# An MLP by Strassen's seven products on one Trainium2 core: the first product also in seven, the hidden layer through DRAM, the second summed over all of K in PSUM

## The chip, the cores and the metric

The kernel runs on one core of a Trainium2 chip. [...] SP's queue (SyncE) issues nearly all DMAs. The metric is device time in us. Each profile tells the span of the instructions; the execution's time is a little longer.

## The reference, cut to what matters

One layer of a hybrid decoder: three token mixers side by side, an output projection, and an MLP. All of it before the MLP stays as it is, so only the end matters:

```
x  = x + y @ w_out[l]                                        # x: 1024 tokens x 1024
hm = rms_norm(x, mlp_norm[l])
x  = x + jnp.square(jax.nn.relu(hm @ mlp_w1[l])) @ mlp_w2[l]  # w1: 1024 x 4096, w2: 4096 x 1024
```

## The kernel before

Every fp32 operand of a matmul is split into a high part (a cast to fp32r, on ScalarE) and a low part (the rest, a subtraction on VectorE or GpSimd). A product is then three matmuls: high x high, high x low, low x high.

The hidden layer's 4096 columns are taken as 32 blocks of 128 or 16 pairs. The tokens form two halves of 512 (`hf`).

First product: `load_w1(ff)` (L1242) loads a block of w1 in two DMAs of 256 KB and splits it. `mlp1(ff, w, hf)` (L1256) sums 8 x 3 matmuls over all of K into one bank, then ReLU on ScalarE and the square on VectorE (L1266); the result `r` stays in SBUF. `hm_split` (L1269) transposes the normalised tokens on TensorE, 32 transposes of 128 x 128 per half, applies mlp_norm's factor, and splits.

Second product: Strassen's seven products of 2 x 2 blocks, for each pair of blocks of K = 256. `COMBO` (L1283) names the sums of `r` blocks (`a_part`, VectorE), the sums of w2 blocks (`b_part`, GpSimd) and where a product goes. `combine` (L1330) makes the sum (L1336), the high part (L1340) and the low part (L1341). `product` (L1355) does 4 x 3 matmuls, three to a bank, and VectorE adds each bank at once to one or two of six sums in SBUF (L1366), 4 x 8 additions of 128 x 512 for each pair.

The loop over pairs (L1400) weaves both: while the pair `pr` goes through the first product (`g1`), the seven products of `pr - 1` run (`g2`). So all of the MLP is one stage. In its last round the sums in SBUF are put together (`total`, L1387) and x1, the residual stream kept in DRAM (`x1d`), is added (`plus_x1`); the last pair is done in 48 + 48 plain matmuls (L1467).

The order in each engine's queue comes from the tile framework: it sorts by the order in the program and by when its own model has operands and buffers ready, and a buffer is given on when its last reader is done. The MLP starts beside the last tile of tokens (`last = att_block(TILES[-1])`, L1297): the transposes and the first 48 matmuls of half 0 stand in its waits. `att_block` (L924) ends by scaling the tile's two halves by the norm's factor (L964) into `xss`.

Of the kernel before, what the change touches and what calls it, by code (L numbers as in the profile page):

```python
# [36 lines left out]
def hymba_trunk(ctx: ExitStack, tc: tile.TileContext, ins: dict, out: bass.AP):  # L37
# [887 lines left out]
    def att_block(i):  # L925
# [37 lines left out]
        for nh in range(2):  # L963
            dve.tensor_scalar(out=xs[nh], in0=x1[:, nh * 512:nh * 512 + 512], scalar1=r, scalar2=None, op0=ALU.mult)  # L964
# [291 lines left out]
    def mlp1(ff, w, hf):  # L1256

        wh, wl = w
        b = cbank(f"m1{ff}{hf}")
        for k in range(NK):  # L1260
            pe.matmul(b, wh[k], hh[hf][:, k, :], start=k == 0, stop=False)  # L1261
            pe.matmul(b, wh[k], hl[hf][:, k, :], start=False, stop=False)  # L1262
            pe.matmul(b, wl[k], hh[hf][:, k, :], start=False, stop=k == NK - 1)  # L1263
        r = mpc.tile([P, 512], F32, tag=f"r{ff % 2}{hf}", bufs=1, name=f"r{ff}{hf}")
        act.activation(out=r, in_=b, func=AF.Relu)  # L1265
        dve.tensor_tensor(out=r, in0=r, in1=r, op=ALU.mult)  # L1266
        return r

    def hm_split(hf, k0, k1):  # L1269

        for k in range(k0, k1):
            b = cbank(f"mT{hf}{k}")
            for j in range(4):
                pe.transpose(b[:, j * P:(j + 1) * P], xss[hf * 4 + j][k // 4][:, k % 4 * P:k % 4 * P + P], ident)
            gk = vec[:, V_MN + k:V_MN + k + 1]
            act.activation(out=hh[hf][:, k, :], in_=b, func=AF.Copy, scale=gk)
            dve.scalar_tensor_tensor(out=hl[hf][:, k, :], in0=b, scalar=gk, in1=f(hh[hf][:, k, :]),  # L1277
                                     op0=ALU.mult, op1=ALU.subtract)
# [4 lines left out]
    COMBO = {  # L1283
# [20 lines left out]
    hid = {}  # L1304
    for ff in range(2):
        hid[h0, ff] = mlp1(ff, wf[ff], h0)
    hm_split(1 - h0, 0, NK)
    for ff in range(2):
        hid[1 - h0, ff] = mlp1(ff, wf[ff], 1 - h0)
    w1_next = load_w1(2)  # L1310
    ctx_b.close()
    yfp.__exit__(None, None, None)
    mpd = ctx.enter_context(opool("mpd"))
    psd = ctx.enter_context(opool("psd", space=PSUM))
    mcnt = [0]

    def mbank(name):
        mcnt[0] += 1
        if mcnt[0] % 2:
            return psd.tile([P, 512], F32, tag="d", bufs=3, name=name)  # L1320
        return cbank(name)
# [178 lines left out]
```

## Time and profile before

| what | value |
|---|---|
| median of 3 runs | 1295.01 us (1294.52 to 1296.42) |
| the profiled execution: time, span | 1294.48 us, 1292.7 us |
| mean granted TensorE clock | 0.994 |
| busy: PE, PEld, DVE, ACT, POOL | 97%, 79%, 80%, 46%, 51% |
| matmuls | 6457 |
| HBM read, written | 66.36 MB, 12.58 MB |

PE is TensorE's matmuls, PEld its weight loads, DVE VectorE, ACT ScalarE, POOL GpSimd, SP the queue of DMA issues. A busy share counts instructions in flight; matmuls overlap, so the distance between starts, not the mean length, is what one costs. "<-" behind a row names what ended the idle time before it. [...]

### The profile page before, as it was taken

To read this page: it belongs to the slowest core of one execution; us is meant where nothing else is said; L and a number is where in the kernel's file an instruction comes from. 1 tells how busy PE (TensorE), PEld (TensorE's weight loads), DVE (VectorE), ACT (ScalarE), POOL (GpSimd) and SP (SyncE) were. 2 spreads that over 40 slices of the span, in tenths; PEclk is the share of its full clock that TensorE was granted. 3 is DMA by queue.
4 is the path that set the end of the run, shared out by engine and by line. 5 is a ranking of instruction groups with operands and counts; after the bars stand their busy time and mean duration, and the time that the engine had idled before them with its cause. 6 is when DMAs were issued, how large, how long until landed. Compare 5 with 4: busy or idle time off the path is not lost.

```text
span 1292.7 us, 18247 instructions
## 1 busy us (share of the span) xinstructions
PE 1248.1 (97%) x6457; PEld 1027.2 (79%) x6457; DVE 1030.9 (80%) x1947; ACT 599.8 (46%) x1283; POOL 659.7 (51%) x581
## 2 busy tenths in 40 slices
PE   5999989989999999999989999999999999999997
PEld 5888779977777777777868888888888888888886
DVE  6899989579989988887757776877677776877797
ACT  6344377357767777765453323333233333233220
POOL 2357434345544555442455555555655546555574
PEclk9999999999999999999989999999999999999999
DMA  5322211112101100013511121111112111111113
GB/s 190 86 72 52 74 44 33 50 50 82 66 33 66 66 33 34 33 50 114 163 57 57 33 65 48 60 58 33 57 50 61 54 41 58 50 57 34 48 50 147
DMA packets 75384, 81.18 MB, mean 63 GB/s; under 512 B 5264, under 2 KB 55580, under 8 KB 75292
## 3 DMA queue, kind: packets, MB, share of 16 engines
q1 hardware_dynamic: 74140, 77.92, 19.1%
q10 hardware_dynamic: 1152, 2.10, 0.5%
q8 instruction: 51, 0.84, 0.3%
q14 instruction: 41, 0.34, 0.1%
HBM read 66.36 MB, written 12.58 MB: 61 GB/s over the span
## 4 chain that ended last, share of the span: by engine, by line
PE 78%; DVE 16%; ACT 3%; issue 2%; POOL 0%; DMA 0%; SPq 0%; ACTq 0%; DVEq 0%; POOLq 0%
PE m L1360 20%; PE m L1261 8%; PE m L1263 8%; PE m L1262 8%; PE t L1125 4%; PE rp L880 3%; PE op L880 3%; PE o L1142 2%; PE o L1146 2%; DVE cv L499 2%; PE ss L1013 2%; PE l L1467 2%; PE sw L1013 1%; PE kv L443 1%; PE kv L444 1%
## 5 line engine op out<-in xcount | busy, mean ns | idle before, releaser
L1366 DVE TENSOR_TENSOR p<-m,p 128x512 f32<-128x512 f32 x240 | 153.2, 678 | 64.5 <-PE m L1360 64.5
L1261 PE MATMUL m<-hh,w1h 128*128 128x512 f32 x512 | 200.5, 392 | 0.0
L1263 PE MATMUL m<-hh,w1l 128*128 128x512 f32 x512 | 200.4, 391 | 0.0
L1262 PE MATMUL m<-hl,w1h 128*128 128x512 f32 x512 | 199.3, 389 | 0.0
L1341 POOL TENSOR_TENSOR bl<-bs,bh 128x512 fp32r<-128x512 f32 x75 | 115.4, 1538 | 134.7 <-ACT bh L1340 130.2
L1360 PE MATMUL m<-bh,ah 128*128 128x512 f32 x420 | 164.6, 392 | 4.6 <-ACT m L1364 4.6
L1366 DVE TENSOR_TENSOR m<-m,m 128x512 f32<-128x512 f32 x224 | 143.3, 680 | 28.0 <-PE m L1360 28.0
L1360 PE MATMUL m<-bl,ah 128*128 128x512 f32 x420 | 164.6, 392 | 0.0
L1360 PE MATMUL m<-bh,al 128*128 128x512 f32 x420 | 164.3, 391 | 0.0
L1336 POOL TENSOR_TENSOR bs<-b,b 128x512 f32<-128x512 f32 x75 | 107.0, 1427 | 16.9 <-DMA b<-in_mlp_w_dram 11.1
L1262 PEld LDWEIGHTS m<-hl,w1h 128*128 128x128 f32 x512 | 96.4, 188 | 21.0
L1263 PEld LDWEIGHTS m<-hh,w1l 128*128 128x128 f32 x512 | 96.2, 188 | 21.0
L1261 PEld LDWEIGHTS m<-hh,w1h 128*128 128x128 f32 x512 | 96.4, 188 | 20.3 <-DVE hl L1277 0.2
L1266 DVE TENSOR_TENSOR r<-r 128x512 f32<-128x512 f32 x64 | 56.0, 875 | 65.3 <-ACT r L1265 65.3
L1251 POOL TENSOR_TENSOR w1l<-w1s,w1h 128x512 fp32r<-128x512 f32 x64 | 83.3, 1303 | 48.0 <-ACT w1h L1250 47.8
L1129 DVE TENSOR_TENSOR pl<-t,ph 128x512 fp32r<-128x512 f32 (+4 forms) x148 | 99.9, 682 | 7.6 <-ACT ph L1128 6.8
L1340 ACT CAST ah<-as 128x512 fp32r<-128x512 f32 x75 | 46.6, 622 | 126.3 <-DVE as L1336 124.2
L1128 ACT CAST ph<-t 128x512 fp32r<-128x512 f32 (+4 forms) x148 | 85.4, 584 | 38.7 <-PE t L1125 30.9
L1360 PEld LDWEIGHTS m<-bh,ah 128*128 128x128 f32 x420 | 79.1, 188 | 22.2 <-ACT m L1364 5.0
L1360 PEld LDWEIGHTS m<-bh,al 128*128 128x128 f32 x420 | 79.1, 188 | 17.1
L1360 PEld LDWEIGHTS m<-bl,ah 128*128 128x128 f32 x420 | 79.1, 188 | 16.9
L1341 POOL TENSOR_TENSOR bl<-b,bh 128x512 fp32r<-128x512 f32 x30 | 46.6, 1554 | 88.0 <-ACT bh L1340 88.0
(459 smaller groups left out, 3088.8 us busy)
## 6 DMA issues: line engine op xcount, KB each, us to landing
w1s<-in_mlp_w_dram SPq DMA_DIRECT2D x64, 256.0 KB
b<-in_mlp_w_dram SPq DMA_DIRECT2D x64, 256.0 KB
wst<-in_w_in_dram SPq DMA_DIRECT2D x32, 256.0 KB
xr<-in_x_dram SPq DMA_DIRECT2D x8, 512.0 KB
x1p<-xr SPq DMA_DIRECT2D x8, 512.0 KB
x<-x1p SPq DMA_DIRECT2D x8, 512.0 KB
x1d<-x SPq DMA_DIRECT2D x8, 512.0 KB
qz<-in_x_dram SPq DMA_DIRECT2D x4, 512.0 KB
```

The costliest lines, as they stand in the source:

```text
L880: pe.matmul(b, a_[:, c * P:(c + 1) * P], w_, start=c == c0 and n == 0, stop=c == c1 - 1 and n == 2)
L1128: act.copy(ph[:kn], tb[:kn])
L1129: dve.tensor_tensor(out=pl[:kn], in0=tb[:kn], in1=f(ph[:kn]), op=ALU.subtract)
L1251: pool.tensor_tensor(out=lo, in0=st, in1=f(hi), op=ALU.subtract)
L1261: pe.matmul(b, wh[k], hh[hf][:, k, :], start=k == 0, stop=False)
L1262: pe.matmul(b, wh[k], hl[hf][:, k, :], start=False, stop=False)
L1263: pe.matmul(b, wl[k], hh[hf][:, k, :], start=False, stop=k == NK - 1)
L1266: dve.tensor_tensor(out=r, in0=r, in1=r, op=ALU.mult)
L1336: sub.tensor_tensor(out=v, in0=raw[terms[0][:2]], in1=raw[terms[1][:2]], op=ALU.add if terms[1][2] == 1 else ALU.subtract)
L1341: lo_on.tensor_tensor(out=lo, in0=v, in1=f(hi), op=ALU.subtract)
L1360: pe.matmul(ps_, a_[:, ts], b_, start=n == 0, stop=n == 2)
L1366: dve.tensor_tensor(out=dst_, in0=ps_, in1=dst_, op=ALU.add)
```

## The change

Both products of the MLP are now done in seven block products, one pass after the other. First pass: for each pair of blocks of w1 (K in two halves, the pair's two blocks, two token halves) `product1(p, m)` does seven products of 4 x 3 matmuls in a variant that reuses banks: three of the products go on summing in a bank that VectorE or ScalarE has read in between. Combinations of w1 blocks (`prep1`) are made on VectorE, for the first two pairs on GpSimd; those of the tokens (`t1` to `t4`) once, half on GpSimd and half on VectorE, and seven operands of 512 x 512 are transposed and split. ReLU and square are both on ScalarE, and the four hidden blocks of a pair are written to DRAM (`hid`). Beside the first pass GpSimd makes the five sums of w2 blocks and they go to DRAM too (`w2s`).

Second pass: one product `m` after the other, each over all 16 pairs, summed in four PSUM banks, with another four for the next product. Each step loads its w2 operand, five steps ahead; hidden blocks are loaded when first needed and stay in SBUF. VectorE adds the four banks to one or two output blocks (`evac2`) once per product; an output block that starts from x1 goes out when its last product is in.

The factors of mlp_norm are now a broadcast row (`gmn`), multiplied in at L964's place. The space set aside for software DMA descriptors is 2048 bytes per partition.

```diff
@@ -885,6 +885,10 @@
+    gmn = att.tile([P, D], F32, name="gmn")
+    nc.sync.dma_start(gmn, ins["mlp_norm"].to_broadcast([P, D]))
...
-            dve.tensor_scalar(out=xs[nh], in0=x1[:, nh * 512:nh * 512 + 512], scalar1=r, scalar2=None, op0=ALU.mult)
+            dve.scalar_tensor_tensor(out=xs[nh], in0=x1[:, nh * 512:nh * 512 + 512], scalar=r, in1=gmn[:, nh * 512:nh * 512 + 512],
+                                     op0=ALU.mult, op1=ALU.mult)
...
+    NPAIR = DFF // (2 * P)
+    hid = {n: [drp.tile([P, 512], F32, name=f"hid{n}{p}") for p in range(NPAIR)] for n in ("11", "21", "12", "22")}
+    W2SUM = {1: ((0, 0), (1, 1), ALU.add), 3: ((0, 1), (1, 1), ALU.subtract), 4: ((1, 0), (0, 0), ALU.subtract),
+             6: ((0, 0), (0, 1), ALU.add), 7: ((1, 0), (1, 1), ALU.add)}
+    w2s = {m: [drp.tile([P, 512], F32, name=f"w2s{m}{p}") for p in range(NPAIR)] for m in W2SUM}
...
+    def load_w1(p):
+        raw1[p] = []
         for j in range(2):
+            r_ = mpc.tile([P, 1024], F32, tag="w1", bufs=4, name=f"w1{p}{j}")
+            nc.sync.dma_start(r_.rearrange("p (k c) -> p k c", k=4),
+                              w1[j * 512:j * 512 + 512, p * 256:(p + 1) * 256].rearrange("(k p) c -> p k c", p=P))
+            raw1[p].append(r_.rearrange("p (k i c) -> p k i c", k=4, i=2))
...
+    def split1(p, name, v, eng):
+        hi = mpc.tile([P, 512], F32R, tag="wh", bufs=5, name=f"wh{name}{p}")
+        lo = mpc.tile([P, 512], F32R, tag="wl", bufs=5, name=f"wl{name}{p}")
+        act.copy(k4(hi), v)
+        eng.tensor_tensor(out=k4(lo), in0=v, in1=f(k4(hi)), op=ALU.subtract)
+        w1c[name, p] = hi, lo
+    def prep1(p, name, eng):
+        if name in ("a11", "a12", "a22"):
+            v = blk(p, int(name[1]) - 1, int(name[2]) - 1)
+        elif name == "s2":
+            s_of["s1", p] = sum1(p, "s1", 2, eng, blk(p, 1, 0), blk(p, 1, 1), ALU.add)
+            v = s_of["s2", p] = sum1(p, "s2", 2, eng, s_of["s1", p], blk(p, 0, 0), ALU.subtract)
+        elif name == "s1":
+            v = s_of.pop(("s1", p))
+        elif name == "s3":
+            v = sum1(p, "s3", 1, eng, blk(p, 0, 0), blk(p, 1, 0), ALU.subtract)
+        else:
+            v = s_of.pop(("s2", p))
+            eng.tensor_tensor(out=v, in0=blk(p, 0, 1), in1=v, op=ALU.subtract)
+        split1(p, name, v, eng)
...
+    def mm1(bank, p, name, cname, start, stop):
+        wh, wl = w1c.pop((name, p))
+        bh, bl = comb[cname]
+        for k in range(4):
+            ks = slice(k * P, k * P + P)
+            pe.matmul(bank, wh[:, ks], bh[:, k, :], start=start and k == 0, stop=False)
+            pe.matmul(bank, wh[:, ks], bl[:, k, :], start=False, stop=False)
+            pe.matmul(bank, wl[:, ks], bh[:, k, :], start=False, stop=stop and k == 3)
...
+    def hidden(p, n, src):
+        t = mpc.tile([P, 512], F32, tag="h11", bufs=2, name=f"h{n}{p}") if n == "11" else src
+        act.activation(out=t, in_=src, func=AF.Relu)
+        act.activation(out=t, in_=t, func=AF.Square)
+        nc.sync.dma_start(hid[n][p], t)
...
+    def product1(p, m):
+        if m == 1:
+            bx[p] = psc.tile([P, 512], F32, tag="x", bufs=2, name=f"x{p}")
+            mm1(bx[p], p, "a11", "b11", True, True)
+            p1s[p] = mpc.tile([P, 512], F32, tag="p1", bufs=2, name=f"p1{p}")
+            act.copy(p1s[p], bx[p])
+        elif m == 2:
+            mm1_more(bx[p], p, "a12", "b21")
+            hidden(p, "11", bx.pop(p))
+        elif m == 6:
...
+        elif m == 7:
+            mm1_more(by_[p], p, "s3", "t3")
+            u3s[p] = ev_tile("u3", 1, f"u3{p}")
+            dve.tensor_tensor(out=u3s[p], in0=by_[p], in1=p1s[p], op=ALU.add)
+            c = ev_tile("c", 3, f"c22{p}")
+            dve.tensor_tensor(out=c, in0=bz[p], in1=u3s.pop(p), op=ALU.add)
+            hidden(p, "22", c)
...
+    def hm_split(name, src, k):
+        hi, lo = comb[name]
+        b = turned(name, src, k)
+        act.copy(hi[:, k, :], b)
+        dve.tensor_tensor(out=lo[:, k, :], in0=b, in1=f(hi[:, k, :]), op=ALU.subtract)
...
+    for p in range(2):
+        load_w1(p)
     last = att_block(TILES[-1])
     next(last)
-    h0 = 1 if TILES[-1] < 4 else 0
-    hm_split(h0, 0, NK)
+    for p in range(2):
+        for n in ("a11", "a12"):
+            prep1(p, n, pool)
+    for name, h in (("b11", 0), ("b21", 1)):
+        for k in range(4):
+            hm_split(name, [xss[t][h] for t in range(4)], k)
     next(last)
     next(last)
     drain(last)
+    for m in (1, 2):
+        for p in range(2):
+            product1(p, m)
...
+    for p in range(2):
+        prep1(p, "s2", pool)
+    with tc.tile_pool(name="tmp2", bufs=1, reuse_waits="tile") as tmp2:
+        t2t = [tmp2.tile([P, 512], F32, name=f"t2t{t}") for t in range(4)]
+        for t in (1, 0, 2, 3):
+            (a_, b_), (c_, d_) = xss[t], xss[4 + t]
+            eng = pool if t in (1, 0) else dve
+            eng.tensor_tensor(out=a_, in0=c_, in1=a_, op=ALU.subtract)
+            eng.tensor_tensor(out=t2t[t], in0=d_, in1=a_, op=ALU.subtract)
+            eng.tensor_tensor(out=c_, in0=d_, in1=c_, op=ALU.subtract)
+            eng.tensor_tensor(out=b_, in0=b_, in1=t2t[t], op=ALU.subtract)
+        for k in range(4):
+            hm_split("t2", t2t, k)
...
+    for m, wn, nxt in ((6, "s1", "t1"), (5, "s3", "t3"), (7, "a22", "t4"), (4, "s4", "b22"), (3, None, None)):
+        for p in range(2):
+            if wn:
+                prep1(p, wn, pool)
+                for k in (2 * p, 2 * p + 1):
+                    hm_split(nxt, SRC[nxt], k)
+            product1(p, m)
+        if m == 7:
+            load_w1(2)
...
+    def w2_sums(p):
+        r_ = []
+        for i in range(2):
+            t = w2p.tile([P, 1024], F32, tag=f"w2r{i}", bufs=1, name=f"w2r{i}{p}")
+            nc.sync.dma_start(t, w2[(2 * p + i) * P:(2 * p + i + 1) * P, :])
+            r_.append(t)
+        for m, (x_, y_, op) in W2SUM.items():
+            o = w2p.tile([P, 512], F32, tag="w2o", bufs=2, name=f"w2o{m}{p}")
+            pool.tensor_tensor(out=o, in0=r_[x_[0]][:, x_[1] * 512:x_[1] * 512 + 512],
+                               in1=r_[y_[0]][:, y_[1] * 512:y_[1] * 512 + 512], op=op)
+            nc.sync.dma_start(w2s[m][p], o)
+            yield
...
+    COMBO1 = {1: "a11", 2: "a12", 3: "s4", 4: "a22", 5: "s1", 6: "s2", 7: "s3"}
+    order1 = []
+    for p in range(2, NPAIR + 1):
+        for d_, m in ((0, 1), (-1, 4), (0, 6), (-1, 3), (0, 5), (0, 2), (0, 7)):
+            if 2 <= p + d_ < NPAIR:
+                order1.append((p + d_, m))
...
+    def prep_to(n):
+        while prepared[0] < min(n, len(order1)):
+            p, m = order1[prepared[0]]
+            prep1(p, COMBO1[m], dve)
+            prepared[0] += 1
+    AHEAD = 4
+    sums = (None for p in range(NPAIR) for _ in w2_sums(p))
+    prep_to(AHEAD - 1)
+    for n, (p, m) in enumerate(order1):
+        if m == 1 and p + 1 < NPAIR:
+            load_w1(p + 1)
+        prep_to(n + AHEAD)
+        next(sums, None)
+        product1(p, m)
+    for _ in sums:
+        pass
...
+    A2 = {1: ("11", "22", ALU.add), 2: ("12", "22", ALU.add), 3: ("11",), 4: ("22",), 5: ("11", "21", ALU.add),
+          6: ("12", "11", ALU.subtract), 7: ("21", "22", ALU.subtract)}
+    DEST = {1: (("11", 1), ("22", 1)), 2: (("21", 1), ("22", -1)), 3: (("12", 1), ("22", 1)), 4: (("11", 1), ("21", 1)),
+            5: (("12", 1), ("11", -1)), 6: (("22", 1),), 7: (("11", 1),)}
+    ORDER2 = (3, 5, 7, 1, 4, 2, 6)
+    steps2 = [(m, q) for m in ORDER2 for q in range(NPAIR)]
+    DONE = {"12": 5, "11": 4, "21": 2, "22": 6}
...
+    def load_res(n, q):
+        t = res[n, q] = rsp.tile([P, 512], F32, tag=f"r{'21' if n == '12' else n}{q}", bufs=1, name=f"r{n}{q}")
+        nc.sync.dma_start(t, hid[n][q])
+    def load_b(i):
...
+        m, q = steps2[i]
+        t = braw[i] = stp.tile([P, 512], F32, tag="b", bufs=6, name=f"b{m}{q}")
+        if m in w2s:
+            nc.sync.dma_start(t, w2s[m][q])
...
+    def prep2(i):
+        if i >= len(steps2):
...
+        m, q = steps2[i]
+        terms = A2[m]
+        v = res[terms[0], q]
+        if len(terms) == 3:
+            v = stp.tile([P, 512], F32, tag="as", bufs=2, name=f"as{m}{q}")
+            dve.tensor_tensor(out=v, in0=res[terms[0], q], in1=res[terms[1], q], op=terms[2])
+        a_ = split2(v, "a", dve, f"{m}{q}")
+        b_ = split2(braw.pop(i), "b", pool if len(terms) == 3 else dve, f"{m}{q}")
+        ready2[i] = a_, b_
+    def evac2(m):
+        for t in range(4):
+            for n, sign in DEST[m]:
+                dve.tensor_tensor(out=acc[n][t], in0=acc[n][t], in1=banks2[m][t], op=ALU.add if sign == 1 else ALU.subtract)
+                if DONE[n] == m:
+                    h, j = int(n[0]) - 1, int(n[1]) - 1
+                    nc.sync.dma_start(outf[(h * 4 + t) * P:(h * 4 + t + 1) * P, j * 512:j * 512 + 512], acc[n][t])
...
+    LEADB, LEADP = 5, 2
+    for i in range(LEADB):
+        load_res("11", i)
+        load_b(i)
+    for i in range(LEADP):
+        prep2(i)
+    for i, (m, q) in enumerate(steps2):
+        load_b(i + LEADB)
+        if m == 3:
+            if q + LEADB < NPAIR:
+                load_res("11", q + LEADB)
+            load_res("21", q)
+            if q == 8:
+                load_acc("12")
+                load_acc("22")
+        elif m == 5:
+            load_res("22", q)
+            if q == 8:
+                load_acc("11")
+        elif m == 1:
+            load_res("12", q)
+            if q == 8:
+                load_acc("21")
+        prep2(i + LEADP)
+        if q == 0:
+            banks2[m] = [pse.tile([P, 512], F32, tag=f"e{ORDER2.index(m) % 2}{t}", bufs=1, name=f"e{m}{t}") for t in range(4)]
+        (ah, al), (bh, bl) = ready2.pop(i)
         for t in range(4):
             ts = slice(t * P, t * P + P)
+            for n, (a_, b_) in enumerate(((ah, bh), (ah, bl), (al, bh))):
+                pe.matmul(banks2[m][t], a_[:, ts], b_, start=q == 0 and n == 0, stop=q == NPAIR - 1 and n == 2)
+        if q == NPAIR - 1:
+            evac2(m)
...
-    nc = _bacc.Bacc("TRN2", target_bir_lowering=False, num_devices=1)
+    nc = _bacc.Bacc("TRN2", target_bir_lowering=False, num_devices=1, dynamic_dma_scratch_size=2048)
```

## Rows read from the trace of the kernel before

**Rows 1.** Busy us and instructions by stretch (A:B us), columns in the first line
```profile
core 0: us, PE busy (x) PEld busy (x) DVE busy (x) ACT busy (x) POOL busy (x), PEclk, DMA share, GB/s
650.00:655.00 5.00, 2.27 (x5) 1.82 (x6) 3.56 (x6) 3.40 (x7) 0.26 (x1) 0.52 0.15 52
...
700.00:1200.00 500.00, 500.00 (x2193) 411.38 (x2192) 374.33 (x585) 157.47 (x269) 281.12 (x197) 1.00 0.17 53
1100.00:1200.00 100.00, 100.00 (x440) 82.30 (x439) 77.26 (x122) 32.13 (x55) 55.56 (x39) 1.00 0.18 56
```

**Rows 2.** The chain that ended last, by engine, whole span
```profile
PE 78%; DVE 16%; ACT 3%; issue 2%; POOL 0%; DMA 0%; SPq 0%; ACTq 0%; DVEq 0%; POOLq 0%
```

**Rows 3.** TensorE by time: start us, length us, engine, line, operation, out<-in
```profile
642.26 0.39 PE L1263 MATMUL m<-hh,w1l 128*128 128x512 f32 x1
642.49 0.39 PE L1261 MATMUL m<-hh,w1h 128*128 128x512 f32 x1
```

**Rows 4.** Groups of instructions, 600 to 1293 us: count, busy us, mean ns, idle before
```profile
L1261 PE MATMUL m<-hh,w1h 128*128 128x512 f32 x512 | 200.5, 392 | 0.0
...
L1360 PE MATMUL m<-bl,ah 128*128 128x512 f32 x420 | 164.6, 392 | 0.0
...
L1366 DVE TENSOR_TENSOR p<-m,p 128x512 f32<-128x512 f32 x240 | 153.2, 678 | 64.5 <-PE m L1360 64.5
...
L1336 POOL TENSOR_TENSOR bs<-b,b 128x512 f32<-128x512 f32 x75 | 107.0, 1427 | 16.9 <-DMA b<-in_mlp_w_dram 11.1
...
L1340 ACT CAST ah<-as 128x512 fp32r<-128x512 f32 x75 | 46.6, 622 | 126.3 <-DVE as L1336 124.2
```

**Rows 5.** By time: the MLP's first matmul, its transposes, the last VectorE instruction
```profile
612.25 0.40 PE L1261 MATMUL m<-hh,w1h 128*128 128x512 f32 x1
...
623.18 0.27 PE L1274 MATMUL mT<-ident,qz 128*128 128x128 f32 x1
...
627.39 0.50 PE L1261 MATMUL m<-hh,w1h 128*128 128x512 f32 x1
...
1288.93 0.69 DVE L1469 TENSOR_TENSOR m<-l,m 128x512 f32<-128x512 f32 x1 [0.67 <-PE l L1467]
```

**Rows 6.** By time: TensorE's two waits and matmuls right behind them
```profile
652.73 0.80 PE L1360 MATMUL m<-bh,ah 128*128 128x512 f32 x1 [4.61 <-ACT m L1364]
...
655.03 0.63 PE L1360 MATMUL m<-bh,al 128*128 128x512 f32 x1
655.46 0.63 PE L1261 MATMUL m<-hh,w1h 128*128 128x512 f32 x1
...
1267.77 0.58 PE L1467 MATMUL l<-bhlast,ah 128*128 128x512 f32 x1 [3.64 <-DVE p L1366]
```

**Rows 7.** By time: the last tile's tokens scaled, GpSimd's first low parts of w1
```profile
603.25 2.51 POOL L1251 TENSOR_TENSOR w1l<-w1s,w1h 128x512 fp32r<-128x512 f32 x2
...
619.67 0.89 DVE L964 TENSOR_SCALAR qz<-x,rm 128x512 f32<-128x512 f32 x2
```

**Rows 8.** By time: GpSimd and VectorE low parts, together and each alone
```profile
643.46 1.75 POOL L1341 TENSOR_TENSOR bl<-b,bh 128x512 fp32r<-128x512 f32 x1
643.97 1.79 DVE L1341 TENSOR_TENSOR al<-as,ah 128x512 fp32r<-128x512 f32 x1
...
652.22 0.69 DVE L1341 TENSOR_TENSOR al<-as,ah 128x512 fp32r<-128x512 f32 x1 [0.68 <-ACT ah L1340]
655.86 1.29 POOL L1341 TENSOR_TENSOR bl<-b,bh 128x512 fp32r<-128x512 f32 x1 [5.60 <-ACT bh L1340]
```

**Rows 9.** Groups by form, 700 to 1200 us: VectorE's low parts
```profile
L1341 DVE TENSOR_TENSOR al<-as,ah 128x512 fp32r<-128x512 f32 x60 | 47.6, 793 | 0.0
```

**Rows 10.** By time, SP's queue: one issue of a 256 KB load
```profile
712.88 0.34 SPq L1327 DMA_DIRECT2D b<-in_mlp_w_dram  x1
```

**Rows 11.** Busy time by stretch, as rows 1: two stretches of many DMAs
```profile
3.00:8.00 5.00, 0.24 (x1) 0.18 (x1) 1.96 (x11) 1.87 (x4) 0.00 (x0) 1.00 0.94 343
...
633.00:640.00 7.00, 7.00 (x33) 5.79 (x32) 5.82 (x4) 4.99 (x9) 5.90 (x4) 1.00 0.76 232
```

More of the change, by code (lines that the diff above doesn't have):

```diff
@@ L1256, in mlp1 @@
[L1256 to L1278, printed above, removed]
@@ new lines, in hymba_trunk, with new_comb, tbank @@
+    w2s = {m: [drp.tile([P, 512], F32, name=f"w2s{m}{p}") for p in range(NPAIR)] for m in W2SUM}
+    hmp = copool("hmp")
+    comb = {}
+    def new_comb(pl, name):
+        comb[name] = [pl.tile([P, 4, 512], F32R, name=f"{name}{s_}") for s_ in "hl"]
+    new_comb(hmp, "b11")
+    new_comb(hmp, "b21")
+    mpc = copool("mpc")
+    psc = ctx_c.enter_context(tc.tile_pool(name="psc", bufs=1, side="right", reuse_waits="tile", space=PSUM))
+    def tbank(name):
+        return psc.tile([P, 512], F32, tag="t", bufs=2, name=name)
@@ new lines, in mm1_more, with turned @@
+    def mm1_more(bank, p, name, cname):
+        wh, wl = w1c.pop((name, p))
+        bh, bl = comb[cname]
+        for k in range(4):
+            ks = slice(k * P, k * P + P)
+            pe.matmul(bank, wh[:, ks], bh[:, k, :], start=False, stop=False, skip_group_check=True)
+            pe.matmul(bank, wh[:, ks], bl[:, k, :], start=False, stop=False, skip_group_check=True)
+            pe.matmul(bank, wl[:, ks], bh[:, k, :], start=False, stop=k == 3, skip_group_check=True)
+    def turned(name, src, k):
+        b = tbank(f"mT{name}{k}")
+        for j in range(4):
+            pe.transpose(b[:, j * P:(j + 1) * P], src[j][:, k * P:k * P + P], ident)
+        return b
@@ L1303, in hymba_trunk @@
     drain(last)
[L1304 to L1310, printed above, removed]
-    ctx_b.close()
-    yfp.__exit__(None, None, None)
[L1313 to L1321, printed above, removed]
@@ new lines, in hymba_trunk, with ybank, zbank @@
+    ctx_b.close()
+    cmt = copool("cmt")
+    for n in ("t2", "t1", "t3", "t4"):
+        new_comb(cmt, n)
+    psd = ctx_c.enter_context(tc.tile_pool(name="psd", bufs=1, side="right", reuse_waits="tile", space=PSUM))
+    def ybank(p):
+        if p % 2 == 0:
+            return psc.tile([P, 512], F32, tag="y0", bufs=1, name=f"y{p}")
+        return psd.tile([P, 512], F32, tag="y1", bufs=1, name=f"y{p}")
+    def zbank(p):
+        return psd.tile([P, 512], F32, tag="z", bufs=2, name=f"z{p}")
@@ new lines, in hymba_trunk, with dpool @@
+    DEST = {1: (("11", 1), ("22", 1)), 2: (("21", 1), ("22", -1)), 3: (("12", 1), ("22", 1)), 4: (("11", 1), ("21", 1)),
[3 more added lines that the diff above has]
+    DONE = {"12": 5, "11": 4, "21": 2, "22": 6}
+    def dpool(name, **kw):
+        return ctx.enter_context(tc.tile_pool(name=name, bufs=1, side="right", reuse_waits="tile", **kw))
+    stp, rsp, pse = dpool("stp"), dpool("rsp"), dpool("pse", space=PSUM)
@@ L1351, in hymba_trunk @@
-    for t in range(4):
-        nc.scalar.dma_start(acc["p11"][t], x1d[t][:, 0:512])
-        nc.scalar.dma_start(acc["p22"][t], x1d[4 + t][:, 512:1024])
-    def product(pr, m, a, b):
+    def prep2(i):
+        if i >= len(steps2):
+            return
+        m, q = steps2[i]
[7 more added lines that the diff above has]
+        ready2[i] = a_, b_
@@ L1356, in product @@
         for t in range(4):
             ts = slice(t * P, t * P + P)
-            ps_ = mbank(f"m2{pr}{m}{t}")
-            for n, (a_, b_) in enumerate(((a[0], b[0]), (a[0], b[1]), (a[1], b[0]))):
-                pe.matmul(ps_, a_[:, ts], b_, start=n == 0, stop=n == 2)
-            for dst in COMBO[m][2]:
-                dst_ = acc[dst][t]
-                if pr == 0 and dst[0] == "m":
-                    act.copy(dst_, ps_)
-                else:
-                    dve.tensor_tensor(out=dst_, in0=ps_, in1=dst_, op=ALU.add)
```

193 lines of the change are left out of this document (58 added, 135 removed), and 7 rows, old and new, of the table COMBO.

## The prediction

> **What bounds the kernel now.** I read the busy time by stretch first. From 700 to 1200 us, the steady part of the MLP, TensorE is busy for 500.00 of 500.00 us at the full granted clock, while VectorE has 374 us, GpSimd 281 us, ScalarE 157 us and the DMA engines a share of 0.17 [rows 1]. The reader should see that only one engine has no slack there. The chain of waits says the same of the whole span: 78% PE, 16% DVE [rows 2]. So in the MLP the time is the number of matmuls times their spacing. TensorE starts 2193 of them in 500 us, but some records may be missing; the timeline gives the spacing directly, 0.227 us from one start to the next (642.26 to 642.49 and on), and I use 0.2273 us, 440 in 100 us [rows 1, 3]. The 0.39 us that a group of matmuls shows as its mean [rows 4] is its pipelined length, not its price.
>
> The MLP's first 512-column matmul starts at 612.25 us, the last VectorE instruction at 1288.93 us, and the span ends at 1292.7 [rows 5]. Between them lie 1536 matmuls of the first product and 1260 + 96 of the second (3 x 512 and 3 x 420 by the groups, one of three shown each [rows 4]; the last pair's 96 by the code), 2892 x 0.2273 = 657 us; the 32 transposes of the second token half, from 623.18 to 627.39, are 4.2 us; that leaves about 15 us of waits. [...]
>
> **Part 1: matmuls removed.** For each of 16 pairs of column blocks the first product took 4 x 24 = 96 matmuls; seven block products with half of K take 7 x 12 = 84: 1344 in all. The second product takes 7 x 16 steps x 12 = 1344 instead of 1356, since the last pair is now also done in seven. 2688 x 0.2273 = 611.0 us against 657.3: 46.3 us less. This is on the path as long as TensorE stays the bound. The matmuls have the same shapes and operand types, so I leave the spacing as it is; the row of weight loads (411 of 500 us busy) shows room under it [rows 1].
>
> **Part 2: transposes added.** Seven operands of 512 x 512 are transposed instead of four: 112 transposes instead of 64. The first 32 stay before 612 us in both. The 80 behind it cost 80 x 4.21/32 = 10.5 us against 4.2 [rows 5]: 6.3 us more, all on TensorE.
>
> **Part 3: the start.** Before, the tokens of the last tile were ready at 620.56 (619.67 + 0.89) and TensorE went straight from the first 48 matmuls into transposes at 623.18 [rows 5, 7]. Now 48 matmuls (products 1 and 2 of pairs 0 and 1) still cover that, but product 6 needs the four differences t2, and two of them are made on GpSimd, behind four low parts, the sums s1 and s2 of both pairs and their low parts. In program order that is 16 GpSimd instructions up to the last t2, from 603.25, where the low parts began before [rows 7]. At 1.29 us with VectorE quiet and 1.75 us with VectorE reading two SBUF operands [rows 8] they end between 623.9 and 631.3. TensorE waits for that from 623.2, plus 0.9 us for the first split. Bounds 0 (some of it moved earlier into GpSimd's idle time) and 9 us; I take 5, since GpSimd is mostly idle just before. The normalisation with mlp_norm folded in is one operand more on VectorE per half tile and the load of that vector is one DMA: I cost them at nothing, hidden by the 10.9 us of matmuls after 612.25; with the cover gone it would be less than one VectorE instruction of this size, 0.69 us [rows 8], twice.
>
> **Part 4: the first pass in its steady state.** A product is 12 x 0.2273 = 2.73 us, a pair 19.1 us. VectorE then has 4 sums and 7 low parts from SBUF and 5 instructions that read PSUM. At the means of the steady part, 0.79 and 0.68 us [rows 9, 4], that is 12.1 us; with every GpSimd sum in its way 11 x 0.69 + 5 x 1.75 + 5 x 0.68 = 19.7 us at the very worst. ScalarE: 7 casts, one copy and 8 passes of ReLU and square at 0.62 each = 9.9 us [rows 4]. GpSimd: 5 sums of w2 at 1.43 = 7.2 us [rows 4]. All are below 19.1 us but the worst VectorE case, which would add 0.6 us in each of 14 pairs; and the operands are prepared four products (10.9 us) ahead, so TensorE should not wait. Two accumulations come back to a bank that VectorE must have read first; the closest has one product, 2.73 us, in between, against 0.68 us plus one instruction in front of at most 1.79. SP issues 13 DMAs per pair at about 0.34 us [rows 10]; a store of w2 sums that waits for GpSimd has the next w1 load queued behind it, which has some 11 us until its use. Cost 0 to 8 us, and I take 0, as the rows of the steady part lie near its better end.
>
> **Part 5: hand-over and second pass.** The first operands of pass two go into space that products 3 to 8 before the end set free, so loads and splits have 8 us; I take 2 us, between 0 and 5. Each step is again 2.73 us. In the five products that sum two blocks VectorE does a sum and a low part, GpSimd one low part; in the other two VectorE does both low parts. VectorE is at 2 x 0.79 = 1.6 us a step, plus the emptying of four banks, up to 8 x 0.68 = 5.4 us in one burst every 16 steps [rows 4, 9]. TensorE has two steps ready (5.5 us) when that burst starts, and the other four banks: about 1 us at each of five hand-overs, bounds 0 and 3, so 5 us. What goes: VectorE's additions of each bank into sums in SBUF, 240 into two of the six alone [rows 4], become 48, but they were off the path.
>
> At this place the trace also shows a conflict. At 643.97 a VectorE low part and, beside it, a GpSimd one at 643.46 take 1.79 and 1.75 us; alone they take 0.69 and 1.29 [rows 8]. Instructions that read one operand from PSUM stay at 0.68 us in a stage where GpSimd is busy 56% of the time [rows 4, 1]. [...]
>
> **The sum.** 612.25 + 611.0 + 10.5 + 5 + 0 + 2 + 5 = 1245.8 us for the last matmul's end, then 3.8 us as now from the last VectorE instruction to the end: span 1249.6. The profiled execution took 1294.48 us for a span of 1292.7, 1.8 more, so 1251.4; the median of the runs lies 0.5 above the profiled one: 1252 us.
>
> **Rivals.** *VectorE and GpSimd take turns in pass two.* If VectorE stands still during every GpSimd instruction, a two-term step takes it 2 x 0.69 + 1.29 + 5.4/16 = 3.01 us against 2.73, in 80 such steps: + 22 us, 1274. For it: [rows 8]. Against: the same mix, one each, ran at 0.79 us in the steady part with GpSimd at 56% [rows 9], so most of the turns were free. *DMA becomes the bound.* Pass one moves 4.46 MB a pair, 233 GB/s; the first two products of pass two need 97 loads of 0.262 MB (37 of w2 or its sums, 48 blocks of the hidden layer, 12 running sums), 25.4 MB in 10.9 + 32 x 2.73 = 98 us, 259 GB/s, with 288 GB/s at its start. The trace has 343 GB/s at a share of 0.94 with large loads, and 232 at 0.76 with loads of this size [rows 11]. If 232 is the ceiling, those loads take 110 us: + 12, 1264. *Slower than before: VectorE sets the pace of pass two.* If its SBUF instructions met GpSimd every time, at 1.75 us, a two-term step would take 2 x 1.75 + 0.34 = 3.84 us: 80 x 1.11 = 89 us, 1341. It binds from a mean of (2.73 - 0.34)/2 = 1.19 us, and decides the sign from 1.46 us (43 us over 160 instructions). For it: the run of 1.7 us rows around 640; against it, that run had GpSimd busy back to back, and here it has one instruction per step. *The change gives its matmuls back* in waits at the start and hand-overs: the upper bounds together (9 + 8 + 5 + 15, less the 12 that I took: 25 us more) give 1277, and no change would need 43.
>
> **Chances.** Forecast, all between 1238 and 1264: 0.58; taking turns 0.11; DMA beyond my terms 0.12; the waits together 0.06; VectorE pacing and slower 0.11; below 1238: 0.02. The low end is the sum without any wait (1240) less 2 us for the earlier stages. The high end, 1285, takes in the first two rivals, nearly both at once, and the waits. About 0.2% is what a measurement tells from no change: faster 0.84, within it 0.04, slower 0.12.
>
> **What would show it.** Right: TensorE busy throughout both passes at full clock, starts 0.227 us apart, 1344 matmuls in each; one wait of some 5 us around 624; the first pass ending near 933 us, the second lasting about 312 us. Wrong: VectorE's two-SBUF instructions in pass two above 1.2 us in the mean; SP or VectorE waits on loads in the first 30 us of pass two; TensorE idle before the accumulations of product 4; a granted clock below 1.00 outside the start.

## The result and the profile after

The changed kernel took 1311.4 us (median of 4 runs, 1310.2 to 1314.2) against 1294.8 in the same comparison: a ratio of 1.0129, 95% interval 1.0111 to 1.0147. It is slower by 1.3%, where the prediction had 1252 us, 3% faster, and a range up to 1285.

The chain of waits of the whole span, by engine, after:

```profile
PE 62%; DVE 13%; DMA 13%; POOL 5%; ACT 3%; issue 2%; SPq 1%; POOLq 0%; ACTq 0%; DVEq 0%
```

Before it had 78% PE and no DMA [rows 2]. DMA and GpSimd are in the chain now, so something other than TensorE sets the pace in part of the MLP. The busy times by stretch (columns as in [rows 1]) say where:

```profile
700.00:800.00 100.00, 86.22 (x358) 69.68 (x356) 59.57 (x71) 39.66 (x67) 47.34 (x34) 0.94 0.73 247
800.00:900.00 100.00, 92.44 (x372) 74.95 (x373) 58.05 (x72) 42.70 (x72) 45.02 (x33) 0.90 0.75 246
1000.00:1050.00 50.00, 50.00 (x215) 41.19 (x214) 29.93 (x44) 20.77 (x36) 5.35 (x4) 0.97 0.90 315
1100.00:1200.00 100.00, 100.00 (x443) 82.86 (x442) 81.89 (x87) 41.67 (x74) 34.66 (x27) 1.00 0.41 132
```

In pass two TensorE starts 443 matmuls in 100 us at the full granted clock, as forecast. In pass one it starts 358 and 372, at a mean granted clock of 0.94 and 0.90. VectorE, ScalarE and GpSimd are at most 60% busy there, and the DMA share is lower than where pass two runs without a gap.

The marks in the timeline (start, length, operation, and in brackets the idle time before it with its releaser):

```profile
627.36 0.40 PE L1314 MATMUL x<-b11h,wha 128*128 128x512 f32 x1
...
649.57 0.69 PE L1380 MATMUL mTt<-ident,t2t 128*128 128x128 f32 x2 [9.34 <-DVE t2t L1428]
...
998.50 0.79 PE L1592 MATMUL e<-bh,ah 128*128 128x512 f32 x1 [3.96 <-ACT bh L1537]
...
1305.50 0.39 PE L1592 MATMUL e<-bh,al 128*128 128x512 f32 x1
```

They divide the 60 us between the forecast end of the last matmul, 1245.8, and the real one, about 1305.7 (the last start, 1305.50, and one spacing). The first MLP matmul is at 627.36 in place of 612.25: 15.1 us. From there to the transposes of t2 it is 22.2 us against 10.9 + 5: 6.3 more. From 649.57 to the end of pass one, 994.5 (998.50 less the wait), it is 345.0 us against 294.6 of matmuls and 10.5 of transposes: 39.9 more. Pass two took 311.2 against 2 + 310.5: 1.3 less. So pass one holds two thirds of the error.

What TensorE waits for there is one thing, eight times. The waits from 690 to 990 us (total, times, longest), of TensorE, VectorE and SP's queue:

```profile
PE y L1372 <- DVE u L1351: 25.0, 8, 4.7
DVE s L1281 <- DMA w<-in_mlp_w_dram: 59.7, 12, 8.1
SPq L1461 <- POOL w2o L1459: 152.9, 77, 7.3
```

TensorE's eight waits are 25.0 of the 39.9 us. Most of the rest is the clock: after the wait of 4.33 us that ends at 755.24, product 4 takes 5.26 us to the next product's first matmul, against 2.72 us for a product at the full clock, and the granted clock is 0.50:

```profile
755.00:760.00 5.00, 4.76 (x11) 3.80 (x12) 2.47 (x4) 2.14 (x4) 1.91 (x2) 0.50 0.86 266
```

Five of the eight waits are followed by a product of 4.4 to 5.3 us, 11.4 us more than at the full clock.

One such wait, followed back in the timeline:

```profile
737.96 0.78 DVE L1290 TENSOR_TENSOR wla<-w,wha 128x512 fp32r<-128x512 f32 x1
738.22 2.02 SPq L1461 DMA_DIRECT2D w2s<-w2o  x2
740.29 0.42 SPq L1455 DMA_DIRECT2D w2r<-in_mlp_w_dram  x1
742.04 0.46 SPq L1455 DMA_DIRECT2D w2r<-in_mlp_w_dram  x1
742.59 1.30 SPq L1269 DMA_DIRECT2D w<-in_mlp_w_dram  x2
749.89 1.73 DVE L1281 TENSOR_TENSOR s<-w,w 128x512 f32<-128x512 f32 x1 [5.98 <-DMA w<-in_mlp_w_dram]
754.42 0.68 DVE L1351 TENSOR_TENSOR u<-y,p 128x512 f32<-128x512 f32 x1
755.24 0.77 PE L1372 MATMUL y<-t4h,wha 128*128 128x512 f32 x1 [4.33 <-DVE u L1351]
```

Read from the bottom: product 4 accumulates into the bank y, which VectorE must have read into u after product 7. That reading stands in VectorE's queue behind the sum s of a pair two further on, which waits 6 us for a w1 load. The load can go out only when the last instruction that reads the same buffer is done. By the times that is the first of the two low parts (wla) before the sum: where SP has no w2 work (below: e2, e9 until 890 us, e10), it sends the load 0.03 us behind it each time. Here that low part is done at 738.74, and VectorE reaches the sum at 743.91, so no 11 us of slack lie between the load and its use. And SP sends the load at 742.59 only, 3.8 us after its buffer is free: it stood before two stores of w2 sums, and two w2 loads went out ahead. 744 to 750 has a DMA share of 1.04 (packets are counted where they start) and 378 GB/s, and the w1 half lands 7.3 us after its issue; VectorE stands through nearly all of that.

The parts differ from pair to pair. In the wait before this one the low part was done at 714.93; the load left SP at 721.05, behind stores that waited for GpSimd, and landed in 3.9 us:

```profile
714.24 0.69 DVE L1290 TENSOR_TENSOR wla<-w,wha 128x512 fp32r<-128x512 f32 x1
719.40 1.56 SPq L1461 DMA_DIRECT2D w2s<-w2o  x2
721.05 0.39 SPq L1269 DMA_DIRECT2D w<-in_mlp_w_dram  x1
724.97 0.69 DVE L1281 TENSOR_TENSOR s<-w,w 128x512 f32<-128x512 f32 x1 [7.88 <-DMA w<-in_mlp_w_dram]
```

Over the eleven such loads from 710 us on, the delay at SP is 0.03 to 6.8 us (3.6 in the mean) and the landing 3.9 to 7.3 us (5.0 in the mean).

### The profile page after: what moved, and what is told of

Its sections match the earlier page's. It is cut to its first block, busy times and chain, and to the rows that moved or that the text cites. A ratio compares the mean times of both kernels' runs of the same rounds, so it can differ in the third digit from the quotient of the medians.

```text
span 1309.7 us, 18671 instructions
## 1 busy us (share of the span) xinstructions
PE 1226.9 (94%) x6301; PEld 1007.6 (77%) x6301; DVE 999.1 (76%) x1729; ACT 676.8 (52%) x1413; POOL 541.2 (41%) x507
## 4 chain that ended last, share of the span: by engine, by line
PE 62%; DVE 13%; DMA 13%; POOL 5%; ACT 3%; issue 2%; SPq 1%; POOLq 0%; ACTq 0%; DVEq 0%
PE e L1592 23%; DMA w2r<-in_mlp_w_dram 6%; DMA w2s<-w2o 5%; POOL w2o L1459 5%; PE t L1130 4%; PE rp L880 3%; PE op L880 3%; PE o L1147 2%; PE o L1151 2%; DVE cv L499 2%; PE ss L1018 2%; PE sw L1018 1%; PE kv L443 1%; PE kv L444 1%; PE sf L1086 1%
## 5 line engine op out<-in xcount | busy, mean ns | idle before, releaser
L1538 POOL TENSOR_TENSOR bl<-b,bh 128x512 fp32r<-128x512 f32 x80 | 109.0, 1363 | 266.4 <-ACT bh L1537 261.0
L1592 PE MATMUL e<-bh,ah 128*128 128x512 f32 x448 | 175.6, 392 | 4.0 <-ACT bh L1537 4.0
L1592 PE MATMUL e<-bl,ah 128*128 128x512 f32 x448 | 175.4, 392 | 0.0
L1592 PE MATMUL e<-bh,al 128*128 128x512 f32 x448 | 175.2, 391 | 0.0
L1549 DVE TENSOR_TENSOR as<-r,r 128x512 f32<-128x512 f32 x80 | 119.2, 1495 | 2.3
L1459 POOL TENSOR_TENSOR w2o<-w2r,w2r 128x512 f32<-128x512 f32 x48 | 65.6, 1381 | 121.5 <-DMA w2r<-in_mlp_w_dram 105.0
L1592 PEld LDWEIGHTS e<-bh,ah 128*128 128x128 f32 x448 | 84.6, 189 | 22.1 <-ACT bh L1537 4.4
L1592 PEld LDWEIGHTS e<-bl,ah 128*128 128x128 f32 x448 | 84.7, 189 | 18.0 <-DVE bl L1538 0.4
L1592 PEld LDWEIGHTS e<-bh,al 128*128 128x128 f32 x448 | 84.6, 189 | 17.4
L1537 ACT CAST bh<-b 128x512 fp32r<-128x512 f32 x112 | 69.1, 617 | 9.0 <-POOL bl L1538 6.9
```

What stands on the lines that cost most here:

```text
L1459: pool.tensor_tensor(out=o, in0=r_[x_[0]][:, x_[1] * 512:x_[1] * 512 + 512], in1=r_[y_[0]][:, y_[1] * 512:y_[1] * 512 + 512], op=op)
L1537: act.copy(hi, v)
L1538: eng.tensor_tensor(out=lo, in0=v, in1=f(hi), op=ALU.subtract)
L1549: dve.tensor_tensor(out=v, in0=res[terms[0], q], in1=res[terms[1], q], op=terms[2])
L1592: pe.matmul(banks2[m][t], a_[:, ts], b_, start=q == 0 and n == 0, stop=q == NPAIR - 1 and n == 2)
```

## The experiments

**Where the 15 us at the start come from.** Edit, e1: the same two lines, later in the code.

```
-    gmn = att.tile([P, D], F32, name="gmn")
-    nc.sync.dma_start(gmn, ins["mlp_norm"].to_broadcast([P, D]))
 ...
     load_wo("rest", 1, halves_of_x1("r"))
+    gmn = att.tile([P, D], F32, name="gmn")
+    nc.sync.dma_start(gmn, ins["mlp_norm"].to_broadcast([P, D]))
```

> Only the place of the broadcast norm row in its pool changes: it is taken after the two x1 buffers instead of before them, so these get the addresses that they had before the change. If the row pushed a buffer onto memory that is released late (the second load of output weights waited 22.2 us for a TensorE matmul, and everything after it ran 7 to 9 us late), that load is issued within 2 us of the first, the first MLP matmul comes 7 to 9 us earlier, and the time falls to 1302 to 1304 us. Rival: the delay comes from the row's own DMA or from the instruction with one more operand; then the time stays at 1309 to 1312.

Measured: 1307.9 us, ratio 1.010 (1.0067 to 1.0132); the first MLP matmul at 620.40, 7.0 us earlier. A load of w_out in SP's queue, after and in e1:

```profile
245.04 23.02 SPq L833 DMA_DIRECT2D wosr<-in_w_out_dram  x2
```

```profile
243.72 0.89 SPq L833 DMA_DIRECT2D wosr<-in_w_out_dram  x2
```

The vector's tile, allocated first in its pool, moved the tiles behind it by 4 KB, and one of the two loads then waited 22 us for an instruction that still used that space. The span of the profiled execution gained 3.5 us of the 7, since pass one lost a little more, and the single runs lie between 1303.4 and 1316.2. The cause of the 7 us is shown; a gain in the total is not clear of the spread.

**Is it the work on w2?** Edit, e2: no w2 sums in pass one, and pass two multiplies single blocks of w2 in their place (that part of the edit isn't shown).

```
-        next(sums, None)
```

> The sums of w2 blocks are left out of pass one, loads and stores of it too; pass two multiplies single w2 blocks in their place. This leaves pass one with w1 loads and the stores of the hidden layer alone. If w2's traffic in pass one is what holds it (through SP's queue or through the DMA engines), TensorE's waits between 680 and 1000 us go from about 33 us to under 8 us and the time falls by 25 to 35 us, to 1277 to 1287. Rival: VectorE's order (sums of w1 ahead of the readings of banks) makes the waits whatever the DMAs do; then at most 10 us go.

Measured: 1272.6 us, ratio 0.982 (0.9804 to 0.9833): 39 us less than the changed kernel. TensorE is busy for 200.00 of 200 us from 700 to 900, the waits for u are gone. So nearly all of the 40 us hang on w2's loads, sums or stores.

**Which part of it?** Three edits. e3 gives w2's raw tiles two buffers each (`bufs=1` to `bufs=2` in w2r). e4 issues w1's loads from ScalarE's queue (`nc.sync` to `nc.scalar` from pair 3 on). e6 leaves out the stores (`nc.sync.dma_start(w2s[m][p], o)`).

> The same work and traffic, but the two w2 rows of a pair are loaded into one of two sets of buffers. Theory: five sums and stores took 15.2 us per pair because the next load waits for the last sum and then takes 6 us, and SP, in order, holds back the w1 loads behind them, so that five products also took 15 us instead of 13.7. Then the pairs of w2 come every 13.7 us or faster and 20 to 28 us go, to 1283 to 1291. Rival: the 16 DMA engines are full at a share of 0.75 and 250 GB/s, so a load takes its 6 to 7 us however early it is issued; then less than 8 us go, 1303 to 1311.

> The w1 loads from the fourth pair on are issued from ScalarE's queue; all else is as in the changed kernel. If SP's order ties w1 to w2, the loads come within 1 us of their buffer being free, w2 alone keeps its pace of 15 us a pair and drops behind, and 15 to 25 us go: 1286 to 1296. If the DMA engines are the limit, under 8 us go. If ScalarE, in order, stands still in front of a load whose buffer is not free, its casts come late and the time rises above 1312.

> The w2 loads and GpSimd's sums stay in pass one, but the sums are not stored, and pass two reads single blocks of w2 in their place (the output differs for that). 1.31 of 4.46 MB a pair leave, and SP no longer waits for GpSimd. Without all of the w2 work it was 1272.6. Theory (late w1 loads, by traffic and by SP standing before a store): 1275 to 1290. Rival (GpSimd's sums in VectorE's way, or the w2 loads by themselves): above 1300, as only the stores have gone.

Measured: e3 1307.9 us, 3.5 less than 1311.4 where its theory had 20 to 28, the DMA share up to 0.83 (so 0.75 was no ceiling) and the waits the same (24.2 us, 8 times). e4 1333.9 (ratio 1.0285): ScalarE's in-order queue stands at the loads in place of SP's (the cast at 760.94 waited 8.0 us, with the load issued at 760.52 ahead of it), waits for u of up to 10.1 us. e6 1357.7, far from my theory; the rival had only "above 1300", and neither had it slower than the changed kernel: with 1.3 MB a pair less to move, pass one got slower (252 to 267 matmuls in 100 us at a DMA share of 0.47 to 0.51). SP's queue in e6 shows why: the next w2 load now stands there for GpSimd, up to 10.9 us at a time, with w1 behind it (640 to 1010 us).

```profile
SPq L1455 <- POOL w2o L1459: 147.0, 30, 10.9
DVE s L1281 <- DMA w<-in_mlp_w_dram: 101.0, 13, 19.9
```

A w1 half whose buffer was free at 717.57 left SP at 732.49, behind the w2 loads of two pairs, and landed in 6.7 us. Fewer bytes and longer waits for w1: bytes are not the limit, and SP's order alone can make w1 late. Why more w2 loads stand ahead of w1 there stays open.

**Is it the slack, or SP's order?** Edits: e5 adds a third pair of w1 buffers, in w2's pool, and loads pair p + 2 in place of p + 1; e9 moves w2's issues.

```
-            nc.sync.dma_start(t, w2[(2 * p + i) * P:(2 * p + i + 1) * P, :])
+            nc.gpsimd.dma_start(t, w2[(2 * p + i) * P:(2 * p + i + 1) * P, :])
 ...
-            nc.sync.dma_start(w2s[m][p], o)
+            nc.gpsimd.dma_start(w2s[m][p], o)
```

> Everything of the changed kernel, with buffers for three pairs of raw w1 in place of two, so that the w1 loads of a pair are issued one pair (about 19 us) earlier. Theory (the w1 load is issued at a moment when it has only a few products left until VectorE's first sum of that pair; under the DMA load of pass one it lands late, the sum stands in VectorE's queue ahead of the reading of the accumulator after product 7, and TensorE waits for that bank): the waits of product 4 for u (25 us, 8 of them) and of VectorE's sum for w1 (63 us) nearly vanish, and the time falls by 25 to 38 us, to 1273 to 1287. Rival (the DMA engines cannot carry pass one's 4.46 MB a pair in 19 us, whatever is issued when): the waits come back elsewhere, the time stays within 8 us of 1311. Second rival (VectorE or GpSimd themselves are too slow beside one another): also no change.

> The w2 loads of pass one and the stores of their sums are issued from GpSimd's queue in place of SP's, so that no w1 load stands behind a store that waits for GpSimd; the traffic is the same. If SP's order alone makes w1 late: 1275 to 1290, and the wait of VectorE's sum for w1 goes under 15 us. If it is the landing time under the DMA load: 1300 to 1315, with the wait still there. Issuing costs GpSimd time of its own, 7 issues a pair, which it has.

Measured, e5: 1300.5 us (ratio 1.0038, 1.0023 to 1.0053), 11 us less than the changed kernel and short of the 25 to 38 of its theory. From 700 to 800 TensorE is busy 98.2 us at the same 247 GB/s; from 800 on it stands again, and VectorE's sum waits for w1 up to 14.7 us. More slack helps for a while and is then used up. e9: 1366.1 us, yet 443 and 441 matmuls in the two stretches of 100 us from 700 to 900, and here the w1 half comes 3.6 us after its issue, which follows the low part at once:

```profile
748.49 1.02 DVE L1290 TENSOR_TENSOR wla<-w,wha 128x512 fp32r<-128x512 f32 x1
...
749.53 2.77 SPq L1269 DMA_DIRECT2D w<-in_mlp_w_dram  x2
...
753.16 0.69 DVE L1281 TENSOR_TENSOR s<-w,w 128x512 f32<-128x512 f32 x1 [1.27 <-DMA w<-in_mlp_w_dram]
...
987.39 0.69 DVE L1363 TENSOR_TENSOR c<-z,u 128x512 f32<-128x512 f32 x1 [85.10 <-DMA hid<-c]
```

The last row is where e9 lost it all: SP stood before a load of pass two's running sums whose space w2's buffers held until 980, and the stores of the hidden layer stood behind it. The landings of e9 before that are 3.6 to 6.7 us; in e2, with no w2 traffic at all, they are 3.6 to 4.0 us (a load at 748.82, its sum at 752.40). What the move took away first of all is the delay at SP: 0.03 us in place of 3.6. In e9's trace the loads that GpSimd issues are a queue of their own beside SP's (2.38 MB in q0, 2.31 MB in q1, 739 to 759 us). The w1 half landed in 7.3 us behind two w2 loads in SP's queue, and in 3.6 us with w2 in the other. Whether it is the bytes sent just ahead in the same queue that make a landing long or the traffic of both queues together, no run takes apart.

**The whole of it.** e10 is e9 with the early running sums loaded from GpSimd's queue as well; e13 is e10 with two buffers for raw w2 and four for its sums.

```
-            nc.sync.dma_start(a_, x1d[h * 4 + t][:, j * 512:j * 512 + 512])
+            (nc.sync if n == '21' else nc.gpsimd).dma_start(a_, x1d[h * 4 + t][:, j * 512:j * 512 + 512])
```

> As e9 (w2's loads and the stores of its sums from GpSimd's queue), and the first three sets of running sums for pass two loaded from GpSimd's queue too. In e9 TensorE was busy 199.9 of 200 us from 700 to 900 with the same traffic as in the changed kernel, then stood 86 us because SP stood before a load of running sums whose space w2's buffers held until 980, with the stores of the hidden layer behind it. Theory (SP's in-order queue is what makes pass one wait, not the traffic and not VectorE beside GpSimd): pass one runs at 443 matmuls in 100 us to its end, the 86 us go, the time is 1268 to 1282, about 35 us under the changed kernel's 1311. Rival (the traffic, only moved): TensorE stands elsewhere in pass one or at the hand-over, 1290 or more.

> e10 with two buffers for each half of raw w2 and four for its sums in place of one and two: the same bytes in a shorter time, so a higher DMA share while they run (0.85 or more, against 0.70), and w2 done before 920. Theory (the traffic is no limit as long as SP is free): within 4 us of e10. Rival (w1's loads land late once the DMA engines are nearly full): the waits of product 4 come back, 8 us or more slower than e10.

Measured, e10: 1281.2 us, ratio 0.987 (0.9816 to 0.9915). Pass one of e10 by stretch, then its hand-over:

```profile
700.00:800.00 100.00, 100.00 (x443) 82.84 (x442) 67.52 (x86) 49.65 (x84) 55.85 (x61) 1.00 0.70 227
800.00:900.00 100.00, 100.00 (x443) 82.84 (x442) 61.66 (x85) 50.79 (x86) 53.53 (x63) 1.00 0.71 232
...
950.00:1050.00 100.00, 85.90 (x354) 69.63 (x353) 63.82 (x72) 38.32 (x66) 47.62 (x53) 0.91 0.86 309
```

Pass one lasts from 649.30 to 955.1, 305.8 us: the forecast's 305.1. From 710 us on, the loads that gate the sums leave SP 0.03 us after their buffer is free and land in 3.6 to 5.0 us. The same work and the same bytes, from two queues in place of one. The 39 us came back as 26 in this execution, because w2's sums end later than pass one now and pass two waits 14.2 us for its operands in three places.

e13 missed: I had it within 4 us of e10, and it took 1330.6. Its waits for u are back (39.1 us, 9 times), but not for w1: VectorE's waits for w1 are 6.3 us from 700 to 900. Its instructions are long. The low parts of the sums (wls) on VectorE, 700 to 900 us, in e2, where GpSimd has nothing to do, after, where it is busy for 92 of 200 us, and in e13, where it is busy for 160:

```profile
L1290 DVE TENSOR_TENSOR wls<-s,whs 128x512 fp32r<-128x512 f32 x42 | 28.9, 687 | 14.3 <-ACT whs L1289 14.1
```

```profile
L1290 DVE TENSOR_TENSOR wls<-s,whs 128x512 fp32r<-128x512 f32 x36 | 31.6, 877 | 5.3 <-ACT whs L1289 5.2
```

```profile
L1290 DVE TENSOR_TENSOR wls<-s,whs 128x512 fp32r<-128x512 f32 x32 | 47.9, 1496 | 0.0
```

So the same wait of product 4 has two causes that can stand for each other: the load that comes late, and VectorE's long instructions beside a GpSimd that is busy for 160 of 200 us. The changed kernel has the first.

**The start.** e7 makes the token differences before product 6 on VectorE, the four t2 first; e11 and e12 are e10 with e1's edit, e7's and more of the first two pairs' operands on VectorE (e12 all; the last two lines of the excerpt are e12's alone).

```
-            eng = pool if t in (1, 0) else dve
-            eng.tensor_tensor(out=a_, in0=c_, in1=a_, op=ALU.subtract)
+            dve.tensor_tensor(out=a_, in0=c_, in1=a_, op=ALU.subtract)
...
-            prep1(p, n, pool)
+            prep1(p, n, dve)
```

> The differences of the tokens before product 6 all on VectorE, the four t2 first, instead of half on GpSimd. Theory (GpSimd's instructions back to back hold up VectorE's small rstd instructions of the last tile, 1.1 to 1.2 us each in place of 0.15): that chain, 631.75 to 642.79 now, shrinks to about 3 to 5 us, the wait before product 6 falls from 9.3 us to 2 to 5, the time falls by 4 to 8 us, to 1303 to 1307. Rival (the chain is long because VectorE's own queue is full, and eight more instructions of 0.7 us make it longer): the wait stays at 9 us or grows, no gain.

> e10 with two more edits: the mlp_norm vector allocated and loaded after the tiles that were there before (as e1), and the token differences and the operands after s2 of the first two pairs prepared on VectorE, so that GpSimd has only the first four low parts and the s2 of two pairs there. Theory (the three losses are separate and add up): 4 to 7 us for the first, 4 to 8 us for the second, 1254 to 1270; this would beat the kernel before. Rival (the start's gain of e7, 2 us, is all there is): 1264 to 1275.

> e11 with the preparations of the first two pairs all on VectorE: GpSimd is quiet while the last tile's chain of small instructions runs on VectorE. If GpSimd's instructions are what holds the small ones up: that chain takes 2 to 3 us in place of 11, the two waits of TensorE before 620 and before product 6 (4 and 9 us) fall to under 4 us together, and it is 3 to 8 us faster than e11. If VectorE's own load is the limit: the same as e11 or slower, by up to 7 us (ten instructions of 0.7 us more).

Measured: e7 1309.5 us, the wait 6.8 in place of 9.3, a gain no larger than the spread. e11 1269.6 (ratio 0.979, 0.9750 to 0.9828), e12 1259.9 (0.973, 0.9686 to 0.9775; single runs from 1256.5 to 1269.7): 51 us faster than the changed kernel, 2.7% faster than the kernel before. In e12's profile the first MLP matmul is at 614.16, in e11's at 620.93. The chain of small instructions for the last tile, after and in e12:

```profile
635.20 0.14 DVE L81 TENSOR_SCALAR rm<-rm 128x1 int32<-128x1 int32 x1
635.38 1.07 DVE L84 TENSOR_TENSOR rm<-rm 128x1 f32<-128x1 f32 x1
636.49 1.22 DVE L85 TENSOR_TENSOR rm<-rm 128x1 f32<-128x1 f32 x1
637.74 1.22 DVE L86 SCALAR_TENSOR_TENSOR rm<-rm 128x1 f32<-128x1 f32 x1
```

```profile
626.26 0.15 DVE L84 TENSOR_TENSOR rm<-rm 128x1 f32<-128x1 f32 x1
626.33 0.69 DVE L1433 TENSOR_TENSOR yf<-yf,t2t 128x512 f32<-128x512 f32 x1
626.93 0.16 DVE L85 TENSOR_TENSOR rm<-rm 128x1 f32<-128x1 f32 x1
```

After, GpSimd is busy for 28.6 of the 30 us from 610 to 640, and seven of the eight small instructions with two operands in SBUF in this tile's chain take 1.07 to 1.24 us; in e12 it has no instruction there and they take 0.15 to 0.16. The wait before t2 stayed, 7.4 us in e12: there VectorE's own queue of 0.69 us instructions stands between the small ones. The total is better, that one wait is as the second theory had it.

## Why the prediction was wrong

**The step that failed is in Part 4**: "a store of w2 sums that waits for GpSimd has the next w1 load queued behind it, which has some 11 us until its use. Cost 0 to 8 us, and I take 0". The mechanism is named there and the size is wrong: 39.9 us. The 11 us were counted from products in the order of the loop. But a load can't go out before its buffer is read for the last time, and that reading is a late low part: in e2 VectorE comes to the sum on the new data 2.7 us behind it (748.78 to 751.50). A load that leaves at once and lands in 3.6 to 5.0 us nearly fits that (e2, e10: waits of VectorE of 0.7 to 2.6 us a pair, hidden from TensorE). The changed kernel's doesn't: SP holds it back by 3.6 us in the mean, as the sentence feared, and it then lands in 3.9 to 7.3 us. What the waits cost was raised once more by the clock (11.4 us behind five of the eight), which the forecast had at full speed throughout. The prediction's own sign of being wrong, TensorE idle before the accumulations of product 4, is what came. e5, e9 and e10 show both halves of it: more slack gives 11 us, a queue of its own gives the pass its full pace. The bound of 8 us was an argument about VectorE's mean load; it held no wait in a queue.

**The start** was carried over: "The normalisation with mlp_norm folded in ... and the load of that vector is one DMA: I cost them at nothing". Its 4 KB moved other tiles, 7.0 us by e1. I had looked at what the load does and not at what it displaces.

**Part 3's wait** was 9.3 us, just beyond its bounds of 0 to 9, with 5 taken; I had priced GpSimd's own queue. What was left out is that VectorE's 128x1 instructions are held up too (1.07 to 1.24 us in place of 0.15 to 0.16), which by e11 and e12 (one execution each) cost 6.8 us ahead of the first matmul; behind it no gain of that size was shown. With e1's 7.0 that is 13.8 of the start's 15.1 us.

**Parts 1, 2 and 5 were right.** 443 matmuls in 100 us at the full clock are 0.226 us each, against the forecast's 0.2273; pass one of e10, transposes included, took 305.8 us against 305.1; pass two took 311.2 us against 312.5, its first wait 4.0 us against 2 (bounds 0 to 5), and the emptying of the banks, taken at 5 us, made TensorE wait nowhere.

**The rivals.** VectorE and GpSimd do meet in pass two: the sums of two blocks take 1.5 us there, against 0.69 us for such a sum in pass one of e2, with GpSimd idle.

```profile
L1549 DVE TENSOR_TENSOR as<-r,r 128x512 f32<-128x512 f32 x80 | 119.2, 1495 | 2.3
L1538 DVE TENSOR_TENSOR al<-as,ah 128x512 fp32r<-128x512 f32 x80 | 59.5, 744 | 19.4 <-ACT ah L1537 19.1
```

With the low part that is 2.24 us a step against 2.73, under the point of 1.19 us in the mean that the text had named: no stall. DMA as the bound is refuted by 315 GB/s without a gap at 1000 to 1050 us, where 232 was the feared ceiling. The rival that was right in kind is the last, waits that give the matmuls back; it was priced at 25 us and 43 were thought out of reach. The slower outcome had been tied to VectorE in pass two alone, so its 0.12 stood on the wrong pass.

## What to carry to other kernels

For a load that reuses a buffer, measure the slack from the last reader of the old data to the first reader of the new, in the engine's own order, and set against it the time that the queue stands before it can send the load, and the landing behind everything that it sends just before; the loop's distance in products says nothing. A queue that carries stores which wait for a slow producer should not carry the loads of another pipeline: moving them gave pass one its 39 us back, of which the later end of w2's sums took 13 at the hand-over. And a new small tile has a place as well as a price.

## What the runs showed of the hardware

A 128x1 VectorE instruction with two operands in SBUF took 1.07 to 1.24 us in seven of eight cases beside a GpSimd that is busy for 9.9 of the 10 us from 630 to 640 (the last tile's chain, after), and 0.15 to 0.16 us beside one without an instruction from 610 to 650 us (e12); with one operand it took 0.14 us in the first and 0.15 in the second. A load of 512 KB from SP's queue landed in 3.6 to 4.0 us with no w2 traffic (e2, a DMA share of 0.34), in 3.6 to 5.0 us with w2's in GpSimd's queue (e10, 0.70), and in 3.9 to 7.3 us with w2's in the same queue (after, 0.73 to 0.75), 7.3 us behind two such loads.
